# TensorE in the program's order through a chunk attention, with the gate and the output projection cut into smaller steps

## The chip, the core and the metric

One core of a Trainium2 chip runs the whole program. The metric is device microseconds of one execution. The engines are TensorE (PE, with its weight loads as PEld), VectorE (DVE), ScalarE (ACT), GpSimd (POOL) and the queue that issues the DMAs (SP).

## The reference

Two transformer-like blocks run one after the other on 512 rows of width 1024, all in float32. Only the first block is touched. It computes, in short:

```
h  = rmsnorm(x) * (1 + sc_m) + sh_m
z, xbc, dt, q, k, v = split(h @ w_in)
y_ssd = rmsnorm(ssd(xbc, dt) * silu(z)) * norm_w      # 512 wide, "the gate" is silu(z)
y_att = softmax(q k^T / 8 + bias, causal by chunks) v  # 8 heads of 64
x  = x + g_m * (concat(y_ssd, y_att) @ w_out)
h  = rmsnorm(x) * (1 + sc_f) + sh_f                    # then a convolutional FFN
```

The vectors sc, sh and g come from c_act @ w_ada, 6 pieces of 1024.

## The kernel before, in words

Activations are held with the feature in the partition: x, and y = concat(y_ssd, y_att), are eight input tiles of 128 x 512 (k = 0 to 7; y's tiles 0 to 3 are the ssd's, 4 to 7 the attention's). Every float32 product of a weight is made of three fp32r products (mm3, L277 to L279): weight and activation are split in a high and a low part, and high x high, low x high and high x low are summed in one PSUM tile. A weight tile (1024 columns, 512 KB) is loaded into `wr`, ACT makes its high part `wh` (L260), DVE the low part `wl` (L261). There are five `wr` and three each of `wh` and `wl`. PSUM has two tiles "d" for such outputs and six tiles "m" for all else.

Four parts of the code matter here.

- **The gate** (L970): for each of four tiles m, 24 products with w_z, tanh on ACT (L973), two DVE multiplications into yS (L975, L976), and a running sum of squares (L346, L348). One gate tile is issued with each of the first four steps of the attention.
- **The attention** (L1002 to L1039): 16 steps s = 4t + i, t the pair of heads, i the block of 128 queries, n = 128(i + 1) keys. `scores` makes two products (L1002) and, for both heads, the softmax: add the bias and take the maximum (DVE, L1007), exp (ACT, L1009), reciprocal and scaling (DVE, L1010, L1011). One step later `values` transposes the probabilities on PE (L1032), ACT copies them to PT (L1033), and after the fourth block of a pair PE multiplies by v (L1039) and ACT and DVE split the result into y's tile 4 + t (L260, L261).
- **The ssd's norm**, placed within the attention: column sums of the squares on PE (L361), a power on POOL (L371), four diagonal matrices on DVE (L380), their product with ones on PE (L381), then y's tiles 0 to 3 (L474 to L476).
- **early_tiles** (L301): the output projection's first three output tiles, called at the last step of the attention. It issues 17 of their 24 triple products, for all input tiles that are there, and returns a function that issues the rest. Behind it come output tiles 3 and 4 one by one, and the last three in a "seam" that cuts the 512 columns in halves and hides the next norm. Its steps also consume the loads of w_ada: 32 DVE accumulations in all (L431, L433), with column sums on PE (L437) after each eight.

A scheduler places the instructions of each engine: it may take an instruction ahead of others of its engine that were written earlier, by its own costs and priorities. So the order on PE in before isn't the order of the code: the early tiles, written behind the last step's scores, start on PE some seven steps earlier. At run time each engine takes its own list strictly in order.

Of the kernel before, what the change touches and what calls it, by code (L numbers as in the profile page):

```python
# [14 lines left out]
ALU = mybir.AluOpType  # L15
# [167 lines left out]
def _prog(ctx, tc, nc, I, out):  # L183
# [114 lines left out]
                    PE.matmul(ps[32 * g : 32 * g + 32], lhsT=w[:, 32 * k : 32 * k + 32], rhs=x[b][:, k, :].bitcast(F32), start=(i + b == 0), stop=(i + b == 2))  # L298
        return ps

    def early_tiles(src, x, *n):  # L301

        w = [parts(raw(src[j])) for j in range(len(n))]
        ps = [psd() if j < 2 else psm() for j in range(len(n))]

        def run(j, k):
            mm3(ps[j], [t[:, k * P : (k + 1) * P] for t in w[j]], [t[:, k, :] for t in x], k == 0, k == 7)

        def rest():
            for j, m in enumerate(n):  # L310
                for k in range(m, 8):
                    run(j, k)
            return ps

        for k in range(7):
            for j, m in enumerate(n):
                if k < m:
                    run(j, k)
        return rest

    def tiles_a(src, js, x, first=None):
# [485 lines left out]
def _mix1(env):  # L807
# [159 lines left out]

    yacc = pt(sm, [P, 512], "acc", bufs=1)

    def gate(m):  # L970
        ps = tile_a(I["w_z"][m], x)
        th = pt(XW, [P, 512], "nh")
        ACT.activation(th, ps, AF.Tanh, scale=0.5)  # L973
        g = pt(XW, [P, 512], "nt")
        DVE.scalar_tensor_tensor(g, th, 1.0, ps, op0=ALU.add, op1=ALU.mult)  # L975
        DVE.scalar_tensor_tensor(yS[:, m, :], g, 0.5, yS[:, m, :], op0=ALU.mult, op1=ALU.mult)  # L976
        sumsq(yacc, yS[:, m, :], m == 0)

    y = []
    yr = []  # L980
    w_out = []


    with tc.tile_pool(name="att", bufs=1, reuse_waits="tile") as M2:

        def bias_tile(h):
            b = pt(M2, [P, 512], "bias", bufs=4)
# [5 lines left out]
        def scores(t, i):  # L993
            if i == 0:
                state[t] = ([pt(M2, [P, 4, 512], "PT", bufs=3) for _ in range(2)], [bias_tile(2 * t), bias_tile(2 * t + 1)])
            _, bias = state[t]
            n = (i + 1) * P
            pss, out = [], []
            for e in range(2):
                ps = psm()  # L1000
                r = slice(64 * e, 64 * e + 64)
                PE.matmul(ps[:, :n], lhsT=qk[r, t, i * P : (i + 1) * P], rhs=qk[r, 4 + t, :n], start=True, stop=True)  # L1002
                pss.append(ps)
            for e in range(2):
                S = pt(M2, [P, 512], "S", bufs=5)
                st = pt(sm, [P, 4], "st", bufs=8)
                DVE.tensor_tensor_reduce(out=S[:, :n], in0=pss[e][:, :n], in1=bias[e][:, 512 - n :], scale=1.0, scalar=-3e38, op0=ALU.add, op1=ALU.max, accum_out=st[:, 0:1])  # L1007
                DVE.tensor_scalar(st[:, 1:2], st[:, 0:1], -1.0, None, op0=ALU.mult)
                ACT.activation(S[:, :n], S[:, :n], AF.Exp, bias=st[:, 1:2], accum_out=st[:, 2:3])  # L1009
                DVE.reciprocal(st[:, 3:4], st[:, 2:3])  # L1010
                DVE.tensor_scalar(S[:, :n], S[:, :n], st[:, 3:4], None, op0=ALU.mult)  # L1011
                out.append(S)
            if t == 0:
                gate(i)
            if (t, i) == (0, 3):
                y.extend(pt(env["HB"], [P, 8, 512], n, F32R) for n in ("hh", "hl"))
            if (t, i) == (1, 2):
                yr.append(env["norm_cols"](512, yacc))
            if (t, i) == (2, 0):
                yr.append(env["rowbc"](yr[0]))  # L1020
            if t == 2:
                env["norm_split"](*y, yS, yr[1], col("ssd_norm_w", 0, 4), (i,))
            if (t, i) == (3, 3):
                w_out.append(env["early_tiles"](I["w_out"], y, 7, 7, 3))
            return out

        def values(t, i, Ss):
# [684 lines left out]
```

## Time and profile before

| | us |
|---|---|
| median of 3 runs (1591.61, 1588.38, 1591.37) | 1591.37 |
| the profiled execution | 1588.89 |
| its span | 1587.1 |
| PE busy | 1550.4 (98%) |
| DVE busy | 850.4 (54%) |
| ACT busy | 524.4 (33%) |
| the attention, with gate and early tiles | about 180 to 261 |

The page's slices are 40 us wide; the stage of interest lies in the fifth to seventh. PE is busy nearly everywhere, by a measure whose ends are modelled, so a wait can lie inside a busy time. The chain of waits, followed back from the end, lies on PE for 90% of the span. In the stage it goes to DVE, ACT, POOL and the w_ada loads.

### The profile page before, as it was taken

The numbers are of one execution on the slowest core, as the hardware profiler recorded it, in microseconds if no ns is written. First come the engines' busy times: TensorE is split into PE (matmuls) and PEld (weight loads), VectorE is DVE, ScalarE is ACT, GpSimd is POOL, SyncE is SP. The second block draws the span as 40 slices with busy tenths as digits, with TensorE's granted clock in tenths as the row PEclk, the third lists the DMA queues.
The fourth block names the chain that finished last, engine by engine and source line by source line (L and its number), as shares of the span: only waits on it lengthen the run. The fifth ranks groups of instructions, "written<-read, shape, count | busy, mean of one in ns | idle before, by whom it ended". The sixth has DMA issues, their size and how long they took to land.

```text
span 1587.1 us, 21111 instructions
## 1 busy us (share of the span) xinstructions
PE 1550.4 (98%) x8208; PEld 1106.1 (70%) x8208; DVE 850.4 (54%) x1679; ACT 524.4 (33%) x964; POOL 35.8 (2%) x33
## 2 busy tenths in 40 slices
PE   8999999999999999989999999999999999999997
PEld 7878857988888888978976688866535545545443
DVE  7777886674564466668467724454242332332333
ACT  4453375442442344443456722231101101101101
POOL 0002000000000000000101000000000000000000
PEclk8999999999999999999999999999999999999999
DMA  8365423333233234402201023497999999999992
GB/s 331 135 197 175 167 73 101 126 100 106 100 94 104 95 93 128 145 18 98 89 27 57 29 86 98 141 316 271 392 369 418 418 415 418 419 417 417 418 417 75
DMA packets 92598, 321.02 MB, mean 202 GB/s; under 512 B 10412, under 2 KB 13100, under 8 KB 91472
## 3 DMA queue, kind: packets, MB, share of 16 engines
q1 hardware_dynamic: 92496, 319.64, 54.1%
q8 instruction: 66, 1.08, 0.3%
q14 instruction: 36, 0.29, 0.1%
HBM read 315.41 MB, written 4.19 MB: 201 GB/s over the span
## 4 chain that ended last, share of the span: by engine, by line
PE 90%; DVE 5%; ACT 2%; DMA 1%; issue 1%; POOL 1%; SPq 0%; DVEq 0%; ACTq 0%
PE d L1522 21%; PE d L277 15%; PE d L278 15%; PE d L279 15%; PE m L1508 4%; PE m L1624 4%; PE m L277 1%; PE m L279 1%; PE m L278 1%; PE m L1219 1%; PE m L1204 1%; DMA wr<-w_ada 1%; PE m L1039 1%; POOL rstd L371 1%; ACT S L1317 1%
## 5 line engine op out<-in xcount | busy, mean ns | idle before, releaser
L1522 PE MATMUL d<-we,xg 128*64 128x512 f32 x1024 | 226.6, 595 | 0.0
L261 DVE TENSOR_TENSOR wl<-wr,wh 128x1024 fp32r<-128x1024 f32 (+1 forms) x148 | 178.1, 1206 | 79.7 <-ACT wh L260 79.1
L277 PE MATMUL d<-bh,wh 128*128 128x512 f32 (+1 forms) x544 | 210.3, 387 | 2.6 <-ACT bh L475 1.5
L279 PE MATMUL d<-bl,wh 128*128 128x512 f32 (+1 forms) x544 | 209.7, 385 | 0.0
L278 PE MATMUL d<-bh,wl 128*128 128x512 f32 (+1 forms) x544 | 209.6, 385 | 0.0
L260 ACT ACTIVATE wh<-wr 128x1024 fp32r<-128x1024 f32 (+1 forms) x148 | 154.0, 1044 | 147.5 <-PE d L279 120.2
L1522 PEld LDWEIGHTS d<-we,xg 128*64 128x64 f32 x1024 | 70.8, 137 | 134.4 <-issue 121.6
L277 PE MATMUL d<-hh,wh 128*128 128x512 f32 (+1 forms) x392 | 147.2, 376 | 0.7 <-ACT bh L845 0.7
L278 PE MATMUL d<-hh,wl 128*128 128x512 f32 (+1 forms) x392 | 145.9, 373 | 0.0
L279 PE MATMUL d<-hl,wh 128*128 128x512 f32 (+1 forms) x392 | 145.8, 373 | 0.0
L277 PEld LDWEIGHTS d<-bh,wh 128*128 128x128 f32 x544 | 102.4, 188 | 25.0 <-issue 2.2
L278 PEld LDWEIGHTS d<-bh,wl 128*128 128x128 f32 x544 | 102.4, 188 | 22.2 <-issue 2.6
L279 PEld LDWEIGHTS d<-bl,wh 128*128 128x128 f32 x544 | 102.6, 189 | 20.1 <-issue 0.5
L1522 PE MATMUL d<-we,aT 128*64 128x512 f32 x512 | 112.6, 592 | 0.7 <-ACT aT L1597 0.7
L1522 PEld LDWEIGHTS d<-we,aT 128*64 128x64 f32 x512 | 36.7, 137 | 73.5 <-issue 71.4
L1625 DVE TENSOR_TENSOR xt<-xt,m 128x512 f32<-128x512 f32 x120 | 73.8, 681 | 22.8 <-PE m L1624 22.8
L277 PEld LDWEIGHTS d<-hh,wh 128*128 128x128 f32 x392 | 73.8, 188 | 16.8 <-issue 2.3
L1608 ACT ACTIVATE yh<-d,ws 128x512 fp32r<-128x512 f32 x32 | 22.0, 688 | 185.2 <-PE d L1522 185.2
L279 PEld LDWEIGHTS d<-hl,wh 128*128 128x128 f32 x392 | 73.7, 188 | 13.7 <-issue 0.5
L278 PEld LDWEIGHTS d<-hh,wl 128*128 128x128 f32 x392 | 73.9, 188 | 12.5
L638 DVE SCALAR_TENSOR_TENSOR cv<-d,cols,cv 128x511 f32<-128x511 f32 x41 | 30.7, 749 | 77.3 <-ACT cv L637 77.3
L1597 ACT ACTIVATE aT<-m 128x512 f32<-128x512 f32 x16 | 9.6, 598 | 176.5 <-PE m L1595 176.5
(430 smaller groups left out, 2631.6 us busy)
## 6 DMA issues: line engine op xcount, KB each, us to landing
we<-w_eg SPq DMA_DIRECT2D x128, 512.0 KB, 9.9
we<-w_eu SPq DMA_DIRECT2D x128, 512.0 KB, 8.9
we<-w_ed SPq DMA_DIRECT2D x128, 512.0 KB, 9.9
wr<-w_up SPq DMA_DIRECT2D x44, 512.0 KB, 3.3
wr<-w_ada SPq DMA_DIRECT2D x32, 512.0 KB, 4.0
wr<-w_out SPq DMA_DIRECT2D x16, 512.0 KB, 3.5
wr<-w_dn SPq DMA_DIRECT2D x16, 512.0 KB, 3.6
wr<-w_mg SPq DMA_DIRECT2D x16, 512.0 KB, 3.3
```

The costliest lines, as they stand in the source:

```text
L260: ACT.activation(hi, src, AF.Copy)
L261: DVE.tensor_tensor(lo, src, hi.bitcast(F32), op=ALU.subtract)
L277: PE.matmul(ps, lhsT=wh, rhs=xh, start=first, stop=False)
L278: PE.matmul(ps, lhsT=wl, rhs=xh, start=False, stop=False)
L279: PE.matmul(ps, lhsT=wh, rhs=xl, start=False, stop=last)
L371: POOL.tensor_tensor(r, ms, mhalf.to_broadcast((P, n)), op=ALU.pow)
L638: DVE.scalar_tensor_tensor(o[:, 1:], ps[:, :511], wc(1), o[:, 1:], op0=ALU.mult, op1=ALU.add)
L1508: PE.matmul(ps[:, :n], lhsT=hx[:, T, d * P : (d + 1) * P], rhs=oh[:, T, :n], start=(T == 0 and hx is hth), stop=(T == 3 and hx is htl))
L1522: PE.matmul(ps[x * m : (x + 1) * m], lhsT=xs[x][:, k, :], rhs=w[k // 2][x][:, k % 2 * 512 : k % 2 * 512 + 512], start=(k == 0), stop=(k == ...
L1608: ACT.activation(yh[:, s], ps, AF.Copy, scale=ws)
L1624: PE.matmul(ps, lhsT=oht[:, T * P : (T + 1) * P], rhs=y[:, s], start=(i == 0), stop=(i == len(mm) - 1))
L1625: DVE.tensor_tensor(xt[:, T, s], xt[:, T, s] if len(done) > 1 else hth[:, T, s].bitcast(F32), ps, op=ALU.add)
```

## The change

Within the attention PE's instructions now stay in the order in which the code issues them (`manual_schedule` for PE); DVE, ACT, POOL and SP are scheduled as before. The gate becomes a generator that yields after four of eight input tiles and at its end. Steps 0 to 2 still issue a whole gate tile, steps 3 and 4 half a tile each. The column sums come at s = 5 instead of 6, the row broadcast at s = 6 instead of 8, the norm's four tiles at s = 7 to 10 instead of 8 to 11. The three early tiles get their weights at s = 5, and one input tile k (nine products, three per output tile) at a time is issued at chosen steps; k = 7 stays for behind the attention.

```diff
-    def early_tiles(src, x, *n):
-        w = [parts(raw(src[j])) for j in range(len(n))]
-        ps = [psd() if j < 2 else psm() for j in range(len(n))]
+    def early_tiles(src, x, *n, steps=None):
+        N = len(n) or 3
+        w = [parts(raw(src[j])) for j in range(N)]
+        ps = [psd() if j < 2 else psm() for j in range(N)]
+        todo = list(range(8))
...
+        def one(k):
+            for j in range(N):
+                mm3(ps[j], [t[:, k * P : (k + 1) * P] for t in w[j]], [t[:, k, :] for t in x], len(todo) == 8, len(todo) == 1)
+            todo.remove(k)
+        def others():
+            while todo:
+                one(todo[0])
+            return ps
+        if steps is not None:
+            steps.append(one)
+            return others
...
-    def gate(m):
-        ps = tile_a(I["w_z"][m], x)
+    def gates():
+        for m in range(4):
+            w = env["parts"](env["raw"](I["w_z"][m]))
+            ps = psd()
+            for k in range(8):
+                env["mm3"](ps, [t[:, k * P : (k + 1) * P] for t in w], [t[:, k, :] for t in x], k == 0, k == 7)
+                if k == 3:
+                    yield
+            env["ada_step"]()
...
-    with tc.tile_pool(name="att", bufs=1, reuse_waits="tile") as M2:
+    with tc.tile_pool(name="att", bufs=1, reuse_waits="tile") as M2, tc.manual_schedule(engines={mybir.EngineType.PE}):
...
-            if t == 0:
-                gate(i)
-            if (t, i) == (0, 3):
+            s = 4 * t + i
+            if s < 5:
+                for _ in range(1 + (s < 3)):
+                    next(fill)
+            if s == 4:
                 y.extend(pt(env["HB"], [P, 8, 512], n, F32R) for n in ("hh", "hl"))
-            if (t, i) == (1, 2):
+            if s == 5:
                 yr.append(env["norm_cols"](512, yacc))
-            if (t, i) == (2, 0):
+                w_out.append(env["early_tiles"](I["w_out"], y, steps=w_out))
+                w_out.reverse()
+            if s == 6:
                 yr.append(env["rowbc"](yr[0]))
-            if t == 2:
-                env["norm_split"](*y, yS, yr[1], col("ssd_norm_w", 0, 4), (i,))
-            if (t, i) == (3, 3):
-                w_out.append(env["early_tiles"](I["w_out"], y, 7, 7, 3))
+            if 7 <= s < 11:
+                env["norm_split"](*y, yS, yr[1], col("ssd_norm_w", 0, 4), (s - 7,))
+            k = {6: 4, 8: 0, 9: 1, 10: 2, 11: 3, 12: 5, 14: 6}.get(s)
+            if k is not None:
+                w_out[1](k)
```

Three places of the orders. First PE around the last step's scores (two products of 512 columns into m475 and m476, in after m487 and m488); k_ident marks a transpose, wh488 and wl489 the third early tile's weights. Before:

```order
L1002 MATMUL m475_2217<-bh107_580 128x512
L1002 MATMUL m476_2219<-bh107_580 128x512
L277 MATMUL m492_2255<-hh356_1820,wh488_2249 128x512
L278 MATMUL m492_2255<-hh356_1820,wl489_2250 128x512
L279 MATMUL m492_2255<-hl357_1821,wh488_2249 128x512
```

The same place in after:

```order
L1031 MATMUL m487_2303<-bh107_580 128x512
L1031 MATMUL m488_2305<-bh107_580 128x512
L1067 MATMUL m493_2321<-k_ident4_92,S481_2272 128x128 x3
L1067 MATMUL m494_2326<-k_ident4_92,S483_2279 128x128 x3
L1067 MATMUL m495_2331<-k_ident4_92,S489_2307 128x128 x4
L1067 MATMUL m496_2337<-k_ident4_92,S491_2314 128x128 x4
L1074 MATMUL m497_2343<-PT458_2188,bl108_581 64x512
```

Before, 24 products of early tiles stand between these scores and the transposes of the last two steps; in after none does.

Second PE from the last early products on; d504 and d510 are output tiles 3 and 4, weights wh502/wl503 and wh508/wl509. Before (the first two early tiles end one row ahead of this piece):

```order
L279 MATMUL m492_2255<-hl357_1821,wh488_2249 128x512
L277 MATMUL m492_2255<-hh356_1820,wh488_2249 128x512
L278 MATMUL m492_2255<-hh356_1820,wl489_2250 128x512
L279 MATMUL m492_2255<-hl357_1821,wh488_2249 128x512
L277 MATMUL m492_2255<-hh356_1820,wh488_2249 128x512
L278 MATMUL m492_2255<-hh356_1820,wl489_2250 128x512
L279 MATMUL m492_2255<-hl357_1821,wh488_2249 128x512
L277 MATMUL m492_2255<-hh356_1820,wh488_2249 128x512
L278 MATMUL m492_2255<-hh356_1820,wl489_2250 128x512
L279 MATMUL m492_2255<-hl357_1821,wh488_2249 128x512
L277 MATMUL d504_2379<-hh356_1820,wh502_2375 128x512
L278 MATMUL d504_2379<-hh356_1820,wl503_2376 128x512
```

The same place in after, from the column sums of w_ada (m512) on:

```order
L455 MATMUL m512_2448<-k_ones7_98,ada274_1458 128x1 x8
L277 MATMUL d391_1926<-hh368_1856,wh383_1910 128x512
L278 MATMUL d391_1926<-hh368_1856,wl384_1911 128x512
L277 MATMUL d392_1927<-hh368_1856,wh386_1916 128x512
L278 MATMUL d392_1927<-hh368_1856,wl387_1917 128x512
L279 MATMUL d391_1926<-hl369_1857,wh383_1910 128x512
L279 MATMUL d392_1927<-hl369_1857,wh386_1916 128x512
L277 MATMUL m393_1928<-hh368_1856,wh389_1922 128x512
L278 MATMUL m393_1928<-hh368_1856,wl390_1923 128x512
L279 MATMUL m393_1928<-hl369_1857,wh389_1922 128x512
L277 MATMUL d504_2382<-hh368_1856,wh502_2378 128x512
L277 MATMUL d510_2420<-hh368_1856,wh508_2416 128x512
```

Between the last product of the first early tile and the first of output tile 3 stood twelve others (two of the second early tile's, ten of the third's); now four stand there. The column sums, which stood behind output tile 4, now come ahead of k = 7.

Third DVE behind the attention: hl is the low part of y's tile 7, xT3 the residual that reads an output tile. Before:

```order
L261 TENSOR_TENSOR hl357_1821<-m497_2329,hh356_1820 128x512
L584 SCALAR_TENSOR_TENSOR xT3_83<-d490_2253,modc11_121,xT3_83 128x512
L584 SCALAR_TENSOR_TENSOR xT3_83<-d491_2254,modc11_121,xT3_83 128x512
L261 TENSOR_TENSOR wl503_2376<-wr501_2373,wh502_2375 128x1024
L261 TENSOR_TENSOR wl509_2414<-wr507_2411,wh508_2413 128x1024
```

In after:

```order
L456 TENSOR_TENSOR modc11_121<-m512_2448,cols1_76 128x8
L620 SCALAR_TENSOR_TENSOR s2516_2464<-modc11_121,cols1_76 128x8
L261 TENSOR_TENSOR hl369_1857<-m497_2343,hh368_1856 128x512
L602 SCALAR_TENSOR_TENSOR xT3_83<-d391_1926,modc11_121,xT3_83 128x512
L602 SCALAR_TENSOR_TENSOR xT3_83<-d392_1927,modc11_121,xT3_83 128x512
L602 SCALAR_TENSOR_TENSOR xT3_83<-m393_1928,modc11_121,xT3_83 128x512
L261 TENSOR_TENSOR wl503_2379<-wr501_2376,wh502_2378 128x1024
```

Ahead of wl503 there now stand three residuals instead of two, and ahead of hl the addition that reads the column sums. SP's list is the same in both kernels but for buffer numbers.

## Rows read from the trace of the kernel before

**Rows 1.** Windows of 5 us: length, busy us and count by engine, PEclk, DMA share, GB/s

```profile
215.00:220.00 5.00, 3.44 (x21) 1.75 (x20) 4.14 (x21) 3.17 (x10) 1.01 (x1) 1.00 0.33 104
250.00:255.00 5.00, 4.98 (x33) 3.65 (x32) 0.00 (x0) 1.85 (x4) 0.00 (x0) 1.00 0.01 3
290.00:295.00 5.00, 3.71 (x29) 3.54 (x30) 4.20 (x11) 3.00 (x8) 0.00 (x0) 1.00 0.77 262
```

**Rows 2.** Timeline of PE: start, us, instruction, in brackets the idle time before it

```profile
209.09 1.07 PE L1039 MATMUL m<-PT,bl 128*64 128x512 f32 x2 [0.84 <-ACT PT L1033]
218.01 0.52 PE L1032 MATMUL m<-k_ident,S 128*128 128x128 f32 x3 [0.89 <-DVE S L1011]
```

**Rows 3.** Chain of waits, 204 to 227: start, us, what

```profile
205.92 0.24 PE d L279
...
216.20 1.02 POOL rstd L371
217.22 0.03 issue
217.25 0.29 DVE diag L380
...
222.77 2.99 PE m L1039 x14
...
226.76 0.24 PE d L277
```

**Rows 4.** Chain of waits, 172 to 182

```profile
175.83 0.23 PE d L277
...
176.53 0.97 PE m L953 x4
```

**Rows 5.** Timeline of ACT, 175 to 258

```profile
175.93 0.38 ACT L948 ACTIVATE bt<-m 128x256 f32<-128x256 f32 x1
...
251.41 1.85 ACT L1033 ACTIVATE PT<-m 128x384 f32<-128x384 f32 x4 [3.47 <-PE m L1032]
...
257.76 1.06 ACT L260 ACTIVATE wh<-wr 128x1024 fp32r<-128x1024 f32 x1 [1.45 <-PE d L279]
```

**Rows 6.** Timeline of PE, 244 to 261

```profile
244.24 1.13 PE L1002 MATMUL m<-bh 64*128 64x512 f32 x4
...
250.88 1.69 PE L1032 MATMUL m<-k_ident,S 128*128 128x128 f32 x14
...
252.82 2.86 PE L1039 MATMUL m<-PT,bl 128*64 128x512 f32 x16
...
260.29 0.40 PE L277 MATMUL d<-hh,wh 128*128 128x512 f32 x1
```

**Rows 7.** Timeline of DVE, 212 to 262

```profile
212.27 1.27 DVE L433 SCALAR_TENSOR_TENSOR ada<-wr,cact,ada 128x1024 f32<-128x1024 f32 x1
...
245.40 0.69 DVE L1007 CUSTOM_DVE_ANT_0 S<-m,bias 128x512 f32<-128x512 f32 x1 [0.43 <-PE m L1002]
...
248.17 0.49 DVE L1011 TENSOR_SCALAR S<-S,st 128x512 f32<-128x512 f32 x1
256.35 0.69 DVE L261 TENSOR_TENSOR hl<-m,hh 128x512 fp32r<-128x512 f32 x1 [7.69 <-ACT hh L260]
257.76 1.41 DVE L584 SCALAR_TENSOR_TENSOR xT<-d,modc,xT 128x512 f32<-128x512 f32 x2 [0.72 <-PE d L279]
259.08 2.46 DVE L261 TENSOR_TENSOR wl<-wr,wh 128x1024 fp32r<-128x1024 f32 x2
```

**Rows 8.** Chain of waits, 270 to 300

```profile
271.35 1.69 PE m L437 x16
273.04 0.02 issue
273.06 0.17 DVE modc L438
273.23 0.66 DVE xT L584
273.89 1.14 DVE wl L261
275.03 0.02 issue
275.05 4.51 DMA wr<-w_ada
```

**Rows 9.** Windows at the start of the experts' stage, columns as in rows 1

```profile
1084.00:1094.00 10.00, 9.38 (x50) 8.25 (x49) 7.02 (x38) 0.61 (x3) 0.00 (x0) 0.89 0.99 368
```

More of the change, by code (lines that the diff above doesn't have):

```diff
@@ L313, in rest, with early @@
             return ps
-        for k in range(7):
+        def early(k):
             for j, m in enumerate(n):
@@ L318, in early_tiles @@
                     run(j, k)
+        def one(k):
[9 more added lines that the diff above has]
+            return others
+        for k in range(7):
+            early(k)
         return rest
@@ L968, in _mix1 @@
     yacc = pt(sm, [P, 512], "acc", bufs=1)
-    def gate(m):
-        ps = tile_a(I["w_z"][m], x)
[L972 to L977, printed above, removed]
+    def gates():
[7 more added lines that the diff above has]
+            env["ada_step"]()
+            th = pt(XW, [P, 512], "nh")
+            ACT.activation(th, ps, AF.Tanh, scale=0.5)
+            g = pt(XW, [P, 512], "nt")
+            DVE.scalar_tensor_tensor(g, th, 1.0, ps, op0=ALU.add, op1=ALU.mult)
+            DVE.scalar_tensor_tensor(yS[:, m, :], g, 0.5, yS[:, m, :], op0=ALU.mult, op1=ALU.mult)
+            sumsq(yacc, yS[:, m, :], m == 0)
+            yield
+    fill = gates()
     y = []
```

## The prediction

> **What bounds the kernel now.** I read the page's chain of waits first. It lies on PE for most of the span, so a wait of PE costs its whole length and the same work in another place costs nothing. Then I read the windows of 5 us through the stage. PE is short of full in one stretch, the middle of the attention, with 1.56 us idle in the 5 us from 215 [rows 1], and again in the seam, 1.29 us from 290 [rows 1]. From 250 on, where the early tiles fill, PE is full while DVE does nothing at all [rows 1]. So before, softmax binds one stretch and PE the next. The timeline names the waits of the first: 0.84 us for the copy of the probabilities, 0.89 us for DVE's scaling [rows 2].
>
> Idle time understates it, since ends of matmuls are modelled. I therefore weighed work against elapsed time. From the end of the last gate product, 205.92 + 0.24 = 206.16, to the first early product at 226.76 [rows 3] lie 20.6 us. The work in them: two products with the values, 2 x 2.99 = 6.0 [rows 3]; 36 transposes at 1.69/14 = 0.12, or 4.3 [rows 6]; six score pairs of together 1664 columns at 1.13/512 each, 3.7 [rows 6]; eight small products of the ssd's norm, for which I estimate 0.2 each, as much as two transposes, 1.7. Together 15.7. PE thus waits 4.9 us there. That is all the change can win in the attention.
>
> **The change part by part.** Loads, splits, tanh, softmax and products are the same in number. Only places change, so every term is a wait that goes or comes.
>
> *The start.* Before, the scheduler puts three products of the first gate tile between the ssd's transposes and the product that waits for their copy: that one starts at 176.53, the fillers at 175.83 [rows 4]. The copy ends at 175.93 + 0.38 = 176.31 [rows 5]. In after the fillers stand behind, and PE waits from 175.83 to about 176.35: +0.5.
>
> *Gate tile 3 in halves, and the middle.* The second half ends one score pair, half a gate tile and no more later. Its tail on DVE meets a neighbour: DVE's list in after has the last accumulation of w_ada (1.27 us, rows 7) ahead of this gate's multiplications, and it waits for a load. Before, it ran only at 212.27 and waited for nothing. So the sum of squares is ready no earlier than its PE column sums, now one step sooner, ask for it. Behind the column sums come POOL's 1.02 us and the diagonals [rows 3], and in DVE's list the softmax of two steps is ahead of these. I follow step by step: PE reaches the row broadcast with only a score pair and two transposes in between, so it stands about 2 us there; at the next n = 512 block (step 7) it has a score pair of 0.3, six transposes of 0.7 and nine products of 2.1 (0.23 each, rows 4) to cover a chain that alone takes 3.3 (below) and shares DVE with the norm's tiles: about 1.4; the copies before the two products with the values, 0.25 and 0.35; the column sums up to 0.2. Together 4.2 against 4.9 before: -0.7. Bounds: -4.9, if every wait there goes, and +1.5, if the load of w_ada arrives late.
>
> *Steps 9 to 14.* Each has nine products and enough work. I take +0.3 for the copies, bounds 0 and +0.6.
>
> *The last two steps.* Softmax of the last step: its first operation starts at 245.40, right behind the scores, and the second head's scaling ends at 248.17 + 0.49 = 248.66 [rows 7], 3.3 us later. Then four transposes, 0.5, and a copy of 1.85/4 = 0.5 [rows 5] stand before the last product can run. That makes 4.3 us from scores to product. Before, 24 early products (24 x 0.23 = 5.5) cover it: scores at 244.24, transposes at 250.88, product at 252.82 [rows 6], no idle time. In after PE has only 14 transposes, 1.7 us, so at least 2.6 us are waited. The lower bound of the wait is 2.0, if the first transposes stretch; the upper 3.2, with ACT's copies of step 14 in between. I take +2.6.
>
> *Behind the attention.* y's tile 7 is split within 1.36 us, from the last product's end at 252.82 + 2.86 = 255.68 to 256.35 + 0.69 = 257.04 [rows 6, 7]; the column sums that now stand here, 1.69 us [rows 8], cover that. But the three early tiles now end together. Output tile 3 needs a buffer of split weights that the first early tile frees, then ACT's 1.06 [rows 5] and DVE's half of 2.46, 1.2 [rows 7]. In DVE's list there stand three residuals (half of 1.41, 0.7 each, rows 7) before it, the third of them for the last early product. From the end of the first early tile: 3 x 0.66 + 1.14 = 3.15 us until output tile 3's second product can start. PE has four early products and two first products of the next tiles, 6 x 0.23 = 1.4. So +1.8. Before, the twelve products in between (2.8 us) met it exactly, up to 260.29 [rows 6]. Bounds: +0.6, if the third residual falls behind, and +2.6, if ACT's square of the residual also delays the weights.
>
> *The seam.* Its wait hangs on DVE: modc at 273.06 waits for the column sums, the weight split ends at 275.03, and only then a w_ada load of 4.51 us starts [rows 8], for which DVE, in order, holds the next norm. The column sums' move takes 1.69 us out of this chain. Against it the weight splits of the next four tiles start later than PE's products, as output tile 3's did: a w_up load goes out only when such a buffer is free, and DVE's list has four such splits before the residual of output tile 4. PE needs that chain at 1.3 us of idle time already [rows 1]. Bounds: -1.6, if the chain gains and the idle time goes, and +1.9, if it is late by all that DVE falls behind. I take +0.9, nearer to the upper, since DVE's order in that place is otherwise unchanged.
>
> *Sum.* +0.5 - 0.7 + 0.3 + 2.6 + 1.8 + 0.9 = +5.4 us. Against the profiled execution, span 1587.1 and 1.8 around it, that is 1588.9 + 5.4 = 1594.3. The profiled one and one of the three runs lie near 1588.6, the two others near 1591.5; the mean of the four is 1590.1, 1.3 below the median. I take the mean as the base: 1590.1 + 5.4 = 1595.5. The bounds give 1590.1 - 3.4 = 1586.7 and 1590.1 + 10.3 = 1600.4.
>
> **The rivals.** *The middle pays the tail back (not slower).* Nine products stand at six of the steps 6 to 12, so all waits of the middle may go: -4.9 instead of -0.7. For it speaks that DVE is 83% busy in the window from 215, not full [rows 1], so its queue could catch up; against it, that the row broadcast sits behind POOL and two softmaxes in a fixed order. The price of the rest stays: 0.5 + 0.3 + 2.6 + 1.8 + 0.9 = 6.1, so +1.2, about 1591.3. It decides from 2.2 us of middle waits on (5.4 - 3.2). If the seam gives back too, -1.6 instead of +0.9, the sum is -1.3, 1588.8; more than 3.2 us below the base needs a tail wait half as long as I count.
>
> The Trainium skill's "Perfetto Trace Analysis", section "Optimization Strategy", speaks for this rival: where the most-contended engine changes over time, interleaving the stretches may help. The trace agrees in its premise, DVE at 0.00 and PE full from 250; by that rule alone the sum would be -4.9 and the time 1585.2.
>
> *The clock falls.* After the 2.6 us at the end PE's granted clock could drop from 2.4 GHz. Against it: with 1.56 us idle of 5 it stayed at 1.00 [rows 1]. For it: a stretch at 0.89 stands behind the lull at the experts' start [rows 9]. At 0.89 a stretch of 10 us costs 1.1; a whole fall to 1.2 GHz doubles the 23 + 24 products of 0.23 behind it, 10.8 us at most. I put 4 more on the sum: 1599.5.
>
> The Trainium skill's "TensorE: Matmul & The Clock Gate", section "HAM oscillation", says that idle gaps in a thin loop take the clock down each time. No run here shows it for a gap of this length; by the rule the time would be this rival's.
>
> *It doesn't do what it says.* PE's order is fixed in the program, as the listed places show; this one has no chance worth a number.
>
> **How the numbers follow.** About 0.2%, 3.2 us, is what a measurement of this kernel can tell from no change. The forecast (slower by 3.2 to 8.5) has 0.54, its own range 1593.3 to 1598.6. The clock 0.06. The middle pays back, within 0.2%: 0.28. Faster by more, the middle and the seam and half of the tail: 0.12. So slower 0.60, same 0.28, faster 0.12. The range reaches from the payback with the seam's gain, 1588.8, to the sum's upper bound, 1600.4.
>
> **What would show it.** In the profile of after: PE idle of 2 us or more between the last scores and the last product with the values, ended by DVE's scaling or ACT's copy; an idle time of 1 to 2 us in front of output tile 3's second product, ended by the weight split on DVE; about 2 us before the row broadcast, ended by a diagonal. The first product of the seam would come at about 277, against 273.04, where the column sums end [rows 8]. I am wrong if the waits of the middle sum to less than 2 us, if PE has under 1 us of idle time before the last product, or if PE's clock leaves 1.00 between 200 and 300.

## The result and the profile after

The changed kernel takes 1605.01 us (median of 4 runs, 1604.28 to 1607.13) against 1591.09 (1588.38 to 1591.61) beside it: a ratio of 1.0094, 95% interval [1.0078, 1.0110], or 13.9 us slower. Measured once more, in a later set of runs, it took 1603.13 (1599.52 to 1606.15) against 1591.78: 1.0073 [1.0056, 1.0091]. The forecast was +5.4 us, 1595.5: the sign was right, the size was not.

The profiled execution's span is 1603.4, 16.3 above that of before. 2.0 of it arise ahead of the change. At the ssd's ten small products, ahead of the changed place, PE is already late, and the first 20 us say why: the same instructions ran at another mean clock. First the two windows (columns as in [rows 1]) and products of before:

```profile
0.00:20.00 20.00, 15.21 (x69) 12.91 (x69) 10.04 (x27) 7.76 (x12) 1.21 (x5) 0.91 0.87 320
```
```profile
172.76 0.87 PE L926 MATMUL m<-mt,X 128*64 128x128 f32 x10
```

and those of after:

```profile
0.00:20.00 20.00, 15.68 (x52) 13.08 (x53) 8.61 (x24) 7.37 (x11) 1.21 (x5) 0.83 0.85 307
```
```profile
174.79 0.87 PE L944 MATMUL m<-mt,X 128*64 128x128 f32 x10
```

Of the 17 profiles of this study nine have 0.91 in this window, and there the ten products begin between 172.8 and 173.4, in one of them at 174.2; eight have 0.83 to 0.85, and begin between 174.4 and 175.2. Up to 170 us the lists of PE, DVE, ACT and POOL are the same in all 17, so I count these 2.0 us as the start's and not the change's. All six kernels that leave PE's order to the scheduler have 0.91, though, and eight of the eleven with PE in the program's order have the lower value; whether that is chance is not shown. So all positions below are counted from the start of these ten products. What is left to explain in these two executions is 14.3 us.

The answers to [rows 1], windows of after:

```profile
215.00:220.00 5.00, 2.38 (x14) 1.39 (x14) 3.77 (x20) 1.59 (x8) 1.01 (x1) 0.80 0.40 134
220.00:225.00 5.00, 4.37 (x15) 3.88 (x16) 3.81 (x13) 2.65 (x6) 0.00 (x0) 0.51 0.00 0
...
260.00:265.00 5.00, 3.32 (x12) 1.79 (x14) 1.67 (x7) 3.11 (x8) 0.00 (x0) 0.74 0.00 0
...
310.00:315.00 5.00, 5.00 (x32) 5.00 (x31) 3.89 (x10) 3.80 (x9) 0.45 (x1) 0.66 0.57 192
```

Read the column PEclk, the granted share of TensorE's full clock of 2.4 GHz, with the busy time. In the second window PE is busy for 4.37 of 5 us and does 15 instructions, at a granted clock of 0.51: it works at 1.2 GHz. Before, the clock was 1.00 in all of the attention. PE's own list of waits, 170 to 320 (line, what it waited for: us in total, times, longest), names these five first:

```profile
PE m L399 <- DVE diag L398: 4.7, 2, 2.5
PE d L277 <- ACT bh L260: 2.4, 1, 2.4
PE m L1067 <- DVE S L1040: 2.2, 2, 1.8
PE d L277 <- ACT wh L260: 1.2, 2, 1.0
PE m L379 <- DVE acc L366: 0.9, 1, 0.9
```

*The middle.* PE, 217 to 224 (columns as in [rows 2]):

```profile
217.38 1.05 PE L1031 MATMUL m<-bh 64*128 64x384 f32 x4 [0.26 <-ACT PT L1068]
220.63 2.04 PE L399 MATMUL m<-diag,k_ones 128*128 128x128 f32 x8 [2.20 <-DVE diag L398]
...
222.90 0.63 PE L278 MATMUL d<-hh,wl 128*128 128x512 f32 x1
223.33 0.63 PE L279 MATMUL d<-hl,wh 128*128 128x512 f32 x1
```

The wait of 2.20 us is the one the forecast put at about 2. Behind it the early products start 0.43 us apart, where [rows 4] give 0.23. DVE, 209 to 221, shows who held the column sums and the diagonals:

```profile
211.39 1.28 DVE L451 SCALAR_TENSOR_TENSOR ada<-wr,cact,ada 128x1024 f32<-128x1024 f32 x1 [1.27 <-DMA wr<-w_ada]
...
218.46 0.56 DVE L1036 CUSTOM_DVE_ANT_0 S<-m,bias 128x384 f32<-128x384 f32 x1 [1.24 <-PE m L1031]
...
220.20 0.67 DVE L398 TENSOR_SCALAR diag<-k_ident,rstd 128x128 f32<-128x128 f32 x3
```

w_ada's accumulation stood 1.27 us for its load and made the column sums late: PE waited 0.87 for them, 0.28 in the second profile of this kernel. But the diagonals stand behind the softmax of the score pair that PE has only just made (218.46): that sets the 2.20, as the run with the accumulation held shows below.

*The tail and output tile 3.* PE, 261 to 275:

```profile
261.32 0.63 PE L1067 MATMUL m<-k_ident,S 128*128 128x128 f32 x4 [1.83 <-DVE S L1040]
262.31 1.07 PE L1067 MATMUL m<-k_ident,S 128*128 128x128 f32 x4 [0.36 <-DVE S L1040]
263.31 3.98 PE L1074 MATMUL m<-PT,bl 128*64 128x512 f32 x16
...
271.87 0.49 PE L277 MATMUL d<-hh,wh 128*128 128x512 f32 x1 [0.23 <-ACT wh L260]
273.34 0.50 PE L277 MATMUL d<-hh,wh 128*128 128x512 f32 x1 [0.97 <-ACT wh L260]
274.01 0.50 PE L278 MATMUL d<-hh,wl 128*128 128x512 f32 x1 [0.18 <-DVE wl L261]
```

The wait is 1.83 + 0.36 = 2.2 us, and the same sixteen products that took 2.86 [rows 6] take 3.98. Output tile 3's weights cost 1.38. Of these 1.20 are booked to ACT's high parts, but the chain of waits goes through DVE, first the three residuals, then the split:

```profile
270.76 2.07 DVE xT L602 x3
272.83 1.13 DVE wl L261
```

*The seam.* Chain of waits, 284 to 305, to compare with [rows 8]:

```profile
288.00 5.24 DMA wr<-w_ada
...
294.35 1.21 DVE ada L451
...
295.57 4.67 DMA wr<-w_ada
...
300.33 1.28 DVE ada L451
...
304.18 0.68 PE m L399 x4
```

Two loads of w_ada, one behind the other, end last; PE waits 2.54 us here. Right behind, it waits 2.44 for the norm's first tile. ACT, 303 to 309, shows why:

```profile
306.21 1.06 ACT L260 ACTIVATE wh<-wr 128x1024 fp32r<-128x1024 f32 x1 [2.15 <-PE m L279]
307.18 1.08 ACT L501 ACTIVATE nh<-nt,modc,s 128x256 f32<-128x256 f32 x2
308.16 0.71 ACT L260 ACTIVATE bh<-nh 128x256 fp32r<-128x256 f32 x2
```

ACT's list has a weight copy, which itself waits for PE, ahead of the norm's tile; before, that copy ran behind it, at 293.99 against 292.08.

### The profile page after: what moved, and what is told of

Read it like the earlier page. It is cut to its first block, busy times and chain, and to the rows that moved or that the text cites. A ratio compares the mean times of both kernels' runs of the same rounds, so it can differ in the third digit from the quotient of the medians.

```text
span 1603.4 us, 21114 instructions
## 1 busy us (share of the span) xinstructions
PE 1557.3 (97%) x8208; PEld 1111.8 (69%) x8208; DVE 851.9 (53%) x1679; ACT 525.2 (33%) x964; POOL 35.8 (2%) x33
## 4 chain that ended last, share of the span: by engine, by line
PE 87%; DVE 6%; DMA 3%; ACT 2%; issue 1%; POOL 0%; SPq 0%; DVEq 0%; ACTq 0%
PE d L1557 21%; PE d L277 14%; PE d L278 14%; PE d L279 14%; PE m L1543 4%; PE m L1659 4%; PE m L279 2%; PE m L277 2%; PE m L278 2%; PE m L1254 1%; PE m L1239 1%; DMA wr<-w_ada 1%; DVE wl L261 1%; ACT S L1352 1%; PE m L1031 1%
```

## The experiments

The table puts all runs on one scale. Each column is how much later PE is than in the kernel before, in us, in the profiled execution: counted from the ssd's ten small products, and less 0.2275 us for each early product more that is done by then (some orders do them sooner). A is the end of the second head pair's products with the values, B of the third's, C of the last's, D the start of the seam's first row broadcast, E the end of w_ada's last column sums near 364 to 380. So A holds the start and the middle, B steps 9 to 14, C the last two steps. The last column is the measured ratio to the kernel before.

```
kernel                                        A     B     C     D     E   ratio
changed                                     3.5   3.2   7.1  12.0  14.1  1.0094
changed, again                              3.5   3.2   7.3  12.3  12.9  1.0073
 + zeros at both places (e1_warm)           0.7   0.4   3.0   8.8   9.5  1.0062
 + zeros, row broadcast only (e16_mid)      2.0   1.7   4.4  10.7  12.7  1.0063
 + zeros, last transposes only (e17_end)    3.0   2.8   5.4  10.4  12.5  1.0066
 + tiles 5, 6 at step 15 (e4_tail)          3.0   3.4   6.8  12.2  14.4  1.0074
 + accumulation held (e3_dve)               2.8   2.5   6.4  12.2  11.9  1.0072
 + third tile held (e6_third)               3.0   2.5   3.6   8.5   9.1  1.0055
 + both held (e12_third_pin)                2.9   2.3   3.4   7.6   7.7  1.0051
 + both held, zeros (e13_all)               0.4  -0.2   2.3   2.9   2.9  1.0028
 PE left to the scheduler (e2_free)        -2.1  -2.4   1.1   5.4   6.1  1.0046
 scheduler, both held (e9_free_third_pin)  -2.0  -2.5  -1.3   1.1   0.9  1.0012
before + program's order (e5_manual)        2.5   7.5  10.6  11.2  11.7  1.0066
before + gate in halves (e10_gate)          0.5   0.9   1.0   0.6   0.7  1.0008
before + one tile per step (e11_out)       -2.0  -2.3   0.3   6.0   8.1  1.0038
 and both held (e15_out_fixed)             -1.6  -2.1  -0.9   2.1   2.2  1.0009
```

**The clock.** Products of zeros, which wait for nothing late, in the two places where PE stood.

```diff
             if s == 6:
+                env["warm"](3)
                 yr.append(env["rowbc"](yr[0]))
...
         def values(t, i, Ss):
             PT, _ = state[t]
+            if (t, i) == (3, 3):
+                env["warm"](3)
```

> The changed kernel with three products of zeros (128x256, fp32) more in two places where PE waits: ahead of the ssd norm's row broadcast, and ahead of the last four transposes of the attention. They read nothing that is late, so no wait of another engine moves. Theory A (the clock): in the profile of after the granted clock is 0.80 and 0.51 in the two windows behind the wait for the diagonals, and the four transposes, the row broadcast (2.04 us against 0.9) and the first six early products (0.43 us each against 0.23) run at half speed; about 2.6 us there and 1.1 in the last products with the values. Kept busy, PE keeps 1.00 and the kernel gains 3 to 4 us of the 14. Theory B (only the waits count, the clock costs nothing that is not hidden): no change within 0.5 us, since the waits stay. If the clock falls in spite of the zeros, the run tells nothing of A's price.

1599.87 us (1597.01 to 1605.15), ratio 1.0062 [1.0045, 1.0079]. The first windows of this kernel, and PE there:

```profile
215.00:220.00 5.00, 4.12 (x24) 2.84 (x25) 3.89 (x23) 2.43 (x9) 1.01 (x1) 1.00 0.33 107
220.00:225.00 5.00, 5.00 (x30) 3.49 (x28) 4.76 (x12) 3.26 (x8) 0.00 (x0) 1.00 0.00 0
```
```profile
217.37 1.56 PE L244 MATMUL m<-zeros 128*128 128x256 f32 x6
219.55 1.16 PE L399 MATMUL m<-diag,k_ones 128*128 128x128 f32 x8 [0.62 <-DVE diag L398]
```

1.56 of zeros and 0.62 idle make the same 2.2 us. The wait has not moved; the clock stays at 1.00, the row broadcast takes 1.16, and column A falls from 3.5 to 0.7. Theory A holds: the price of the middle is 2.8 us, work at half speed behind the wait. In the end the run gains 2 to 5 us, by which of the two measurements of the changed kernel it is set against. Each place by itself, beside the changed kernel on the same chip (the diff is one half of that above):

> The changed kernel with three products of zeros ahead of the row broadcast alone. Theory A (the middle's loss is the clock that falls there, the wait itself stays): granted clock 1.00 from 215 to 225, the first product with the values of the second head pair ends 2.8 us sooner against the ssd's last products than in after, and the whole gains 2.5 to 3.5 us; the tail's wait and slow clock stay. Theory B (what is won in the middle is waited for later, at the attention's tail or in the seam): under 1 us.

> The changed kernel with three products of zeros ahead of the last four transposes alone. Theory A: the transposes and the last products with the values run at full speed, 3.1 us for the products instead of 3.98, the gain 1 to 2 us. Theory B (PE then only waits longer for output tile 3's weights and the seam's loads): under 0.5 us.

> The changed kernel once more, as the base for the runs beside it: 1604 to 1606 us, the granted clock again near 0.8 and 0.5 in the two windows from 215 to 225.

Row broadcast only: 1600.55 (1599.67 to 1604.30), 2.6 below the changed kernel's 1603.13, by medians whose intervals overlap. It is not the clean test that was wanted: in its profile the clock fell sooner, 0.69 from 215 to 220, over a wait for the column sums, so A came down by 1.5 and not by 2.8. Last transposes only: 1602.23 (1599.64 to 1604.63). From B to C it loses 2.6 instead of 3.9 and 4.1; sized so, the clock is 1.3 to 1.5 of the tail. The 0.9 us in the time is too little to tell from none. The changed kernel again showed 0.87 and 0.50 in the two windows, as expected; its time, 1603.13, came 0.9 below the range.

The profile with zeros at the row broadcast only holds the better test of the tail. Nothing was changed there, the wait is the same to 0.01 us, and yet the clock stayed at 1.00:

```profile
255.00:260.00 5.00, 2.81 (x19) 1.50 (x15) 2.97 (x11) 3.06 (x8) 0.00 (x0) 1.00 0.00 0
```
```profile
258.41 0.63 PE L1068 MATMUL m<-k_ident,S 128*128 128x128 f32 x4 [1.82 <-DVE S L1040]
...
259.99 3.12 PE L1075 MATMUL m<-PT,bl 128*64 128x512 f32 x16
```

The last products take 3.12 instead of 3.98, and from B to C it loses 2.7. So the clock's part of the tail is 1.2 to 1.4 by this profile too, and the same wait does not always take the clock down.

**The tail.** More early products in front of the last transposes:

```diff
-            k = {6: 4, 8: 0, 9: 1, 10: 2, 11: 3, 12: 5, 14: 6}.get(s)
-            if k is not None:
+            for k in {6: (4,), 8: (0,), 9: (1,), 10: (2,), 11: (3,), 15: (5, 6)}.get(s, ()):
                 w_out[1](k)
```

> The changed kernel with input tiles 5 and 6 of the three early tiles held back from steps 12 and 14 to step 15, so that 18 products (18 x 0.23 = 4.1 us) stand between the last scores and the last transposes. Theory A (the tail is a wait for softmax that only early products cover): the 1.83 us wait for DVE's scaling and most of the slow clock behind it go, -2.5 to -3.7 us, of which up to 1 us may come back as a wait at step 12 for ACT's copy. Theory B (the wait only moves: behind the attention the three tiles end together all the same and output tile 3's weights are the next limit): -1 or less.

1602.78 (1600.23 to 1605.36), 1.0074 [1.0059, 1.0089]. PE's waits from 240 to 270, and a window:

```profile
PE m L1066 <- DVE S L1040: 1.5, 2, 1.0
PE m L1073 <- ACT PT L1067: 1.3, 2, 1.0
```
```profile
255.00:260.00 5.00, 5.00 (x15) 2.77 (x16) 3.49 (x13) 2.63 (x8) 0.00 (x0) 0.66 0.00 0
```

The wait moved to steps 12 to 14, and the fallen clock with it: C is 6.8 against 7.1. Theory B is nearer, though the place is another: the products have to come from somewhere, and the steps that gave them had none to spare.

**DVE's accumulation.** Held behind the attention, in `ada()`:

```diff
-            DVE.scalar_tensor_tensor(acc, r, cact[:, k : k + 1], acc, op0=ALU.mult, op1=ALU.add)
+            (tc.keep_in_program_order if (j, k) == (4, 7) else id)(DVE.scalar_tensor_tensor(acc, r, ...))
```

> The changed kernel with one instruction of DVE held in the program's place: the last accumulation of w_ada's fifth block (1.27 us, which in after waits 1.27 us for its load in front of gate tile 3's multiplications) stands behind the attention again, and with it its column sums stand behind output tile 4, as in the kernel before. Theory A (DVE held by this load makes the 2.2 us wait for the diagonals, and the wait makes the clock fall; and the column sums in front take cover from the seam's chain): middle -3 to -3.7, seam -2 to -4, together 1597 to 1600. Theory B (the row broadcast waits for POOL and two softmaxes anyway, and the seam is late because the split weights are): -1.3 at most for the middle and 0 for the seam, 1604.

1601.57 (1599.78 to 1603.65), 1.0072 [1.0059, 1.0086]. DVE no longer stands for the load, the column sums come sooner, and yet:

```profile
217.64 2.05 PE L399 MATMUL m<-diag,k_ones 128*128 128x128 f32 x8 [2.20 <-DVE diag L398]
```

The wait is 2.20 to the hundredth, and the broadcast takes 2.05: the clock has fallen. My theory A fails on the middle: what fixes the wait is the softmax between the score pair and the diagonals in DVE's list, which starts with that pair. It gained 0.7 there by the column sums. In the seam the wait for the norm's tile fell to 1.2, but D stays at 12.2.

**The third early tile.** It does its first three input tiles with the others, and the last five where the rest is called for:

```diff
         def one(k):
             for j in range(N):
-                mm3(ps[j], ..., len(todo) == 8, len(todo) == 1)
-            todo.remove(k)
+                if j < 2 or len(todo[2]) > 5:
+                    mm3(ps[j], ..., len(todo[j]) == 8, len(todo[j]) == 1)
+                    todo[j].remove(k)
...
```

> The changed kernel with the third of the three early tiles held back: it does its first three input tiles with the others and its last five behind the attention, 15 products, as in the kernel before. Theory A (the three tiles that end together free their weight buffers together, so output tile 3's weights, the w_up loads behind them and the seam's w_ada loads all start late): the 1.2 us wait for output tile 3's weights goes, the seam's row broadcast comes 2 us sooner after the last product with the values, but four steps of the attention have six products instead of nine, and may wait 1 to 2 us more in sum; -1.5 to -3 in all. Theory B (the seam is late because DVE and the w_ada loads are, whatever the buffers): the seam keeps its 2.5 us wait at the row broadcast and 2.4 at the norm's tile; 0 to +2.

1599.84 (1598.66 to 1601.41), 1.0055 [1.0042, 1.0069]: 3 us gained or more, and not for the reason given. The rest is written outside the part where PE's order is fixed, so the scheduler was free to put nine of the held products in front of the last product with the values. They filled the tail: from B to C this kernel loses 1.1 us, the changed one 3.9. The wait for output tile 3's weights went too, but from C to D it loses 4.9 us like the changed kernel: PE came sooner and waited 1.96 for the diagonals, 2.43 for the norm's tile. On the seam theory B is right.

With the accumulation held too, by the edit of e3_dve:

> The changed kernel with the third early tile held back (three input tiles early, five late) and with DVE's accumulation of w_ada's fifth block held behind the attention, so that its column sums follow output tile 4 again. The run with the third tile held back alone came to 1599.8, the one with the accumulation held alone to 1601.6. Theory A (where the column sums stand sets the seam's wait for the norm's first tile, 2.44 us in each profile with the sums in front and 1.10 to 1.23 in each with them behind): -1.3 us from 1599.8, and the wait reads 1.1 to 1.2; so 1598.5. Theory B (the seam is as late as the loads of w_ada that fly beside w_up's, 5.24 and 6.73 us against 4.51): the norm's wait may shrink, but the row broadcast comes as late; 1599 to 1601.

1598.43 (1594.58 to 1601.90), 1.0051 [1.0035, 1.0067], by its interval no different from the 1.0055 with the third tile alone. PE's wait for the norm's tile is 1.22, as theory A had it, the one for the row broadcast 0.62. ACT from 301 to 304:

```profile
301.38 1.09 ACT L504 ACTIVATE nh<-nt,modc,s 128x256 f32<-128x256 f32 x2 [2.00 <-DVE nt L502]
302.37 0.71 ACT L260 ACTIVATE bh<-nh 128x256 fp32r<-128x256 f32 x2
...
303.29 1.04 ACT L260 ACTIVATE wh<-wr 128x1024 fp32r<-128x1024 f32 x1
```

Here the weight copy stands behind the norm's tile. That, and not the column sums, goes with the wait: the next kernel has the sums in the same late place, the copy in front again (296.50 against 297.46), and the wait of 2.44. In all 17 profiles the rule holds: 2.43 or 2.44 in the ten with the copy in front, 1.10 to 1.23 in the seven with it behind. Theory A's wait came out, for another reason than the one given.

And the zeros of e1_warm on top:

> As the one with the third tile and the accumulation held back, and three products of zeros ahead of the row broadcast and ahead of the last transposes. If the causes found add up: the clock stays at 1.00 from 200 to 270, which is worth some 3 us (the run with the zeros alone gained 5.1 of 14, of which the tail's part is partly had by the third tile's products now): 1594.5 to 1596. What stays over the kernel before is then the start (0.5), the rest of the tail's wait and the seam. Rival: the zeros only move the wait to the seam, where DVE and the w_ada loads set the end: no gain against the run without zeros (1598 to 1600).

1594.49 (1592.77 to 1596.80), 1.0028 [1.0014, 1.0041], 3.9 below the run without zeros on the same chip. The causes add up in the time: with PE still in the program's order, 4.3 us are left of 11 to 14. The zeros did more than keep the clock, though. With them the scheduler put three of the held products, not nine, ahead of the last product with the values, so from B to C this kernel loses 2.5, where the one without zeros loses 1.1; and from C to D it loses 0.6 instead of 4.2, which is not explained here. The rival, that the wait moves to the seam, fails.

**PE's order.** In the changed kernel it is given back to the scheduler:

```diff
-    with tc.tile_pool(name="att", ...) as M2, tc.manual_schedule(engines={mybir.EngineType.PE}):
+    with tc.tile_pool(name="att", ...) as M2:
```

> The changed kernel with PE's order left to the scheduler in the attention, as before the change; the halved gates and the one-input-tile-per-step products stay as written. The scheduler puts fillers back at the start of the attention and mixes early products with the row broadcast; no product is left for it between the last scores and the last products with the values, and the column sums of w_ada still stand ahead of the last early products. Theory A (the program's order on PE makes the loss in the middle): start 0.5 and middle 3.7 us come back, so 1600 to 1601; the tail (2.6 and 1.8 predicted, 3.7 and 2.4 seen) and the seam stay. Theory B (the new places of the work, whoever orders it, make the loss): 1603 to 1605.

1597.91 (1593.59 to 1598.42), 1.0046 [1.0033, 1.0059]. Theory A, and more than I put (1600 to 1601): not only is the middle's loss gone, the place is won, A is -2.1. The scheduler puts early products between the column sums, the diagonals and the transposes, and the clock stays at 1.00 up to 250. The tail loses 3.5 instead. With the third tile and the accumulation held as well (the edits of e6_third and e3_dve beside this one):

> The changed kernel with PE's order left to the scheduler, the third early tile held back and w_ada's accumulation held behind the attention. The scheduler puts nine of the third tile's products between the last scores and the last product with the values. Theory A (program's order, uncovered tail and seam are three separate causes): from the run with the free order (1597.9) -2 for the tail and -1.3 to -3 for the seam, 1593 to 1594.5. Theory B (free order and late third tile pay for the same wait): 1597 to 1598.

1592.31 (1590.19 to 1593.41), 1.0012 [1.0003, 1.0020]. Theory A. Up to the last product with the values this kernel is 1.3 us ahead of the kernel before, and the seam takes that back. Its chain there, 276 to 292:

```profile
276.33 4.47 DMA wr<-w_ada
...
283.14 4.49 DMA wr<-w_ada
```

The loads have the length of [rows 8] again.

**The parts alone.** The kernel before with one part of the change each. First PE's order:

```diff
-    with tc.tile_pool(name="att", ...) as M2:
+    with tc.tile_pool(name="att", ...) as M2, tc.manual_schedule(engines={mybir.EngineType.PE}):
```

> The kernel before with one part of the change: PE runs the attention in the program's order, gates whole, the early output products where the text has them (all 51 behind the last scores). Theory A (a fixed order pays only for the cover that it takes away): the tail is covered by 51 products instead of 24, but the 27 that the scheduler had put between steps 8 and 14 are gone from there, so PE waits for softmax in each of these steps, with the clock falling in some of them; the sum +4 to +10 us, 1594 to 1600. Theory B (PE was never short in those steps, the total of its work is the same): +0.5 for the start only, 1590.5.

1601.59 (1600.41 to 1603.59), 1.0066 [1.0053, 1.0080]: theory A, half a us beyond its upper end (+10.5 by the ratio). With all 51 early products behind the last scores PE waits in each step, and the clock falls twice:

```profile
230.00:235.00 5.00, 3.16 (x11) 0.84 (x9) 3.73 (x19) 3.09 (x10) 0.00 (x0) 0.85 0.01 3
245.00:250.00 5.00, 3.55 (x10) 1.58 (x11) 3.51 (x17) 2.46 (x10) 0.00 (x0) 0.71 0.00 0
```

Then the gate in halves, with `gates()` as in the change:

```diff
-            if t == 0:
-                gate(i)
-            if (t, i) == (0, 3):
+            s = 4 * t + i
+            if s < 5:
+                for _ in range(1 + (s < 3)):
+                    next(fill)
+            if s == 4:
                 y.extend(...)
```

> The kernel before with one part of the change alone: the ssd's gate in halves over five steps; PE's order left to the scheduler, the norm and the early tiles where they were. Theory A (the halving by itself moves only half a gate tile, nothing that waits): within 1 us of the kernel before. Theory B (the late gate tile makes the norm late, and so the row broadcast): +2 to +4.

1591.41 (1588.51 to 1594.76), 1.0008 [0.9998, 1.0018]: theory A, the halves cost nothing that can be measured. But the clock fell in its profile, though PE's order is the scheduler's and the longest wait ahead of the fall is 1.12 us:

```profile
215.00:220.00 5.00, 3.86 (x14) 1.76 (x14) 3.82 (x22) 2.77 (x10) 1.12 (x1) 0.69 0.08 33
```
```profile
216.28 1.00 PE L1045 MATMUL m<-k_ident,S 128*128 128x128 f32 x4 [1.12 <-DVE S L1022]
```

The same window of the kernel before had 1.56 us idle, in pieces of at most 0.89, and kept 1.00 [rows 1, 2].

Then the early tiles, with `early_tiles` as in the change:

```diff
-            if (t, i) == (1, 2):
+            if s == 5:
                 yr.append(env["norm_cols"](512, yacc))
-            if (t, i) == (2, 0):
+                w_out.append(env["early_tiles"](I["w_out"], y, steps=w_out))
+                w_out.reverse()
+            if s == 6:
                 yr.append(env["rowbc"](yr[0]))
...
+            k = {6: 4, 8: 0, 9: 1, 10: 2, 11: 3, 12: 5, 14: 6}.get(s)
+            if k is not None:
+                w_out[1](k)
```

> The kernel before with another part of the change alone: the output projection's three tiles one input tile per step, and the norm's steps one or two earlier; gates whole, PE's order left to the scheduler. Theory A (this part takes the cover from the last step and lets three tiles end together): tail 2.6 to 3.7, behind it 1.8 to 2.4, seam 1 to 3, together +6 to +8, the most of what the whole change costs without the program's order (1597.9). Theory B (the parts cost only together): +2 or less.

1597.23 (1593.64 to 1598.98), 1.0038 [1.0025, 1.0051]: theory A. PE's waits there, 245 to 270, are those of the changed kernel, this time with the clock at 1.00, and from B to C it loses 2.6:

```profile
PE m L1055 <- DVE S L1029: 2.2, 2, 1.8
PE d L277 <- ACT wh L260: 1.2, 2, 1.0
```

And this with the edits of e6_third and e3_dve:

> The kernel before with the output projection's early tiles one input tile per step, gates whole, PE's order left to the scheduler, the third early tile held back and w_ada's accumulation held behind the attention. Counted by work done, the free run with gates whole was level with the kernel before up to the last product with the values (+0.4 us) and lost its 6 us behind it. Theory A (the loss behind the attention is that of the two things held back here): 1590 to 1592.5, no worse than the kernel before. Theory B (the loss stays in the seam, since w_up's loads come late whatever is held back): 1595 to 1597.

1591.77 (1589.49 to 1595.32), 1.0009 [1.0000, 1.0019]: theory A. No run beats the kernel before. The two best versions of the change are slower than it by at most 0.2%, both without the program's order.

## Why the prediction was wrong in size

Term by term, the 14.1 us of the changed kernel's profile (column E) are 8.7 more than the +5.4: 3.7 more in the middle, 1.3 in the last two steps, 0.6 behind the attention and 3.7 in the seam, less 0.6 in steps 9 to 14. Some 4 us of this are the clock, which the sum left at full speed.

*The start, +0.5.* Right: PE waits 0.53 us for the copy, and not at all where the scheduler has the order.

*The middle, -0.7.* The step that failed. It set 4.2 us of waits against 4.9 and let the work behind them run at full speed. The waits came out a little smaller: 0.36, 0.87, 0.26, 2.20, and nothing at step 7, 3.7 in all (3.1 in the second profile). Without the start's 0.5, A says +3.0. In the two kernels whose clock stayed up, A less the start is +0.2 and -0.1: so the waits were counted to within 0.9 us, and 2.5 to 2.8 us (the changed kernel against the one with zeros, and the one with both held against the same with zeros) are the same instructions at 1.2 GHz. I had this mechanism as a rival, with a chance of 0.06, at the other end of the attention, because 1.56 us idle of 5 had left the clock at 1.00 [rows 1]. That was one profile, and it proved little. In all seven profiles with the wait of 2.20 left empty, the clock fell behind it or in it; in the two where zeros took most of it and nothing ahead had pulled the clock down, it did not.

What decides it is not shown. It is not the length of one empty piece alone: the kernel before had pieces of at most 0.89 us [rows 2] and kept its clock, but the one with the gate in halves lost it with no piece longer than 1.12. The tail's wait, 1.83 and 0.36, took the clock down in four profiles and left it up in two; the seam's wait of 2.43 or 2.44 was followed by a fall within 2 us in five profiles of ten.

The Trainium skill's "TensorE: Matmul & The Clock Gate", section "HAM oscillation", which I named beside this rival, tells of a thin loop whose waits, longer than these, take the clock down in every turn. The traces agree that a wait can do it, seven times in seven at 2.20 us, but not that it does so each time.

*That the middle pays the tail back* was the other large rival. The gain is there, 1.6 to 2.5 us in columns A and B, but only when the scheduler mixes the products in; in the program's order nine products stand just behind the broadcast that PE waits for.

*Steps 9 to 14, +0.3.* -0.3 from A to B: no loss.

*The last two steps, +2.6.* Measured 3.9 and 4.1. The wait was 2.2, within the bounds, and ended as foretold. The clock added 1.3 to 1.5 by the run with zeros there; where it stayed up without zeros the same wait lost 2.6 and 2.7, which is what the term had.

*Behind the attention, +1.8.* Output tile 3's weights: 1.38 us, the mechanism right. The chain has 2.07 + 1.13 = 3.20 us where the forecast had 3.15 (its terms add up to 3.12). From C to the seam's first product PE loses 2.4. PE's first product of the seam comes at 284.58 against 273.04 [rows 8]: with 2.0 for the start of the execution, 9.5 late where the terms so far gave 4.5.

*The seam, +0.9, at most 1.9.* Measured 4.6 and 3.1 in the two profiles (E less the 9.5 and 9.8 at the seam's first product). PE waits 2.54 at the row broadcast against 0.47, at the end of a chain in which two loads of w_ada took 5.24 and 4.67 us, where [rows 8] have 4.51, and DVE's splits and sums stand between; 1.3 is ACT's order; the first profile has a window at 0.66 behind these waits, which the second does not show. I had priced what DVE falls behind, and neither the length of the loads nor ACT. What of C to D is loads and what is DVE's list was not taken apart: holding the accumulation alone left D as it was, with the third tile held too it fell by 0.9, with zeros by 4.7 more. That part of the cause stays open.

*The base.* Runs of one kernel spread over 3 to 8 us here. Between profiles of different kernels the start makes 2 of them and the fallen clock's places some more; what makes the spread within one kernel is not shown.

*The signs.* All three waits that were to show the forecast came: 2.20 before the row broadcast, 2.2 in the tail, 1.38 at output tile 3. So did one of the signs of being wrong, the clock that left 1.00 between 200 and 300.

## What to carry to other kernels

Price a wait of TensorE at its length, and, with a good chance, the work behind it at half clock: in the middle 2.2 us cost nearly 5, in the tail 2.6 where the clock stayed up and up to 4.1 where it fell. One profile in which the clock stayed up does not tell that it will. Before fixing an engine's order by hand, look at what the scheduler had mixed into that stretch: the order alone cost 10.5 us, with no instruction more. And work that is moved ahead to fill one stretch is missing where it stood: follow it to the loads, buffers and copies that were timed to it.

## What was not expected of the hardware

The clock's mean over the first 20 us differs between profiles whose instructions there are the same, 0.91 or 0.83 to 0.85, and with it the position by some 2 us. What decides it stays open. A wait of 2.2 us with PE busy on both sides took the clock to 1.2 GHz for some 7 us, the idle part included (0.20 and 0.49 short of full in two windows of 5 us); 1.56 us of zeros in it were enough to keep it in two kernels. The wait of the same length in the tail was followed by a fall in four profiles and by none in two others. And a load of w_ada of the same size took 4.2 to 6.7 us in the seam, 6.73 in the run with the third tile held.
